# Chunked heads in pairs, unnormalised probabilities, outputs transposed on TensorE: one hybrid encoder layer

## The chip, the cores and the metric

The kernel runs on one NeuronCore of one Trainium2 chip. The metric is the device time of one execution in microseconds (us), the median of several runs. Five engines work side by side and meet only at semaphores: PE (TensorE: weight loads and matmuls), DVE (VectorE), ACT (ScalarE), POOL (GpSimd) and SP (SyncE), which here issues the DMA transfers.

## What is computed

One encoder layer over 1024 tokens of width 1024, all in float32. The mixer has two groups of eight heads. The latent group (MLA) has heads of 96 channels for query and key and sees all keys up to the query's chunk of 64 tokens. The chunked group (CA) has heads of 64 channels, sees a band of nine chunks and adds a bias by relative position. Both outputs are concatenated, projected and added to the residual; a gated MLP with a causal convolution follows.

```python
# latent heads, for a block of 128 queries
s = jnp.einsum('bqhd,bkhd->bhqk', qi, k, preferred_element_type=jnp.float32) * scale
s = jnp.where(mask[None, None], s, NEG_INF)          # key chunk <= query chunk
p = jax.nn.softmax(s, axis=-1).astype(v.dtype)
o = jnp.einsum('bhqk,bkhd->bqhd', p, v)
# chunked heads, for a chunk of 64 queries and its band of 576 keys
s = jnp.einsum('bqhd,bkhd->bhqk', qch, kb, preferred_element_type=jnp.float32) * scale + bias[None]
s = jnp.where(valid[None, None, None, :], s, NEG_INF)
p = jax.nn.softmax(s, axis=-1).astype(vb.dtype)
o = jnp.einsum('bhqk,bkhd->bqhd', p, vb)
mixed = jnp.dot(jnp.concatenate([o_mla, o_ca], axis=-1), w_out[l])
x = x + g_a[:, None, :] * mixed
```

## The kernel before

Every float32 product is made of three products of halves (hi*hi, hi*lo, lo*hi); `gemm3` (L144) issues them and its lines L148 to L150 stand for all large projections. `hi_of` (L73, on ACT at L75 or POOL at L77) and `lo_of` (L81, L82) split an operand. `scale_pool` (L70, L71) is POOL's multiplication by a column.

The kernel has four stages in time. First x is normalised and projected for the first head pair. Then the 64 query tiles of the chunked heads and the 64 of the latent heads run (128 queries of one head each), with other products between them. Then comes the output projection of the latent heads with the second norm (from L834), and last the MLP (from L887).

*The attention.* A `Unit` (L626) is four query tiles of one head: eight chunked heads and eight latent ones, in two halves g of the sequence, 32 units. `scores` (L634) makes the tile's score products (L656) in one of two PSUM tiles of tag "S" (two banks each); a chunked tile of the second half has 640 keys in two segments, six products, and one of the first half 128 to 512 keys, three products. Chunked heads lie on 64 partitions: head 2p on 0 to 63, head 2p+1 on 64 to 127 of the same page. DVE masks (L663, L674) and takes the minimum (L667, L671, L675), for scores carry a minus sign; ACT takes the exponential and its row sum (L681) into a tile of tag "P" (three buffers) or, if wider than 640, of tag "pg" (six, shared with other pages). DVE takes the reciprocal of the row sum and scales it (L683, L684). POOL writes the high half-precision part times that column (L698), DVE the low part (L701), both into one of three "HL" buffers; SP issues a transposing DMA (L703) into one of three "PT" buffers. `values` (L707) runs three tiles later (DEPTH): V, with hi and lo side by side in 128 columns, is stationary, the transposed probabilities move, and the result has the 64 channels (twice) on the partitions and 128 queries along the columns (L714). After four tiles ACT and DVE add the two halves with the scale of V undone (L721, L722), and SP stores 64 rows of 512 to DRAM (L723) as `oT_d`.

*The fill products.* The projections of the next pairs, the latent block, the up projections of the latent heads ("up0", "up1") and the chunked heads' output projection ("oca", `f_oca`, L596) are generators that `fill_step` (L777) advances; `pace` (L803) lets R_CA or R_MLA ns of fill run for each ns of attention, and `need` (L794) forces those that a unit must have. `gemm3_f` (L156) ties a fill product behind the attention's product of four entries ago in `trail` (LAG). `f_oca` loads the weights of one half of the columns, reads `oT_d` in slices of 128 tokens (L602), splits them on ACT and POOL (L603, L604) and keeps the result in DRAM (L609). The order on every engine is made by a planner that simulates a timeline; `high_priority` moves scores, splits and values ahead of fill.

*The output projection of the latent heads* (L855 on) reads `oT_d` in slices again (L858), splits them (L859, L860), multiplies, adds the kept part of the chunked heads (L868) and so on through the second norm.

`qk_page` (L612) transposes four token tiles on PE into a PSUM tile of tag "T" (one buffer), and ACT (L619 or L622) and DVE (L620 or L623) split it into a page of tag "Q" or "K".

## Time and profile before

| | us |
|---|---|
| median of 3 runs | 1521.95 |
| the runs | 1520.9, 1521.95, 1524.99 |
| span of the profiled execution | 1526.0 |
| score products of the chunked heads (L656) | 104.3 to 396.8 |
| score products of the latent heads (L656) | 433.0 to 660.0 |
| last products of probabilities and values (L714) | 681.0 |
| output projection of the latent heads on PE | 686.8 to 745.8 |
| first product of the MLP | 793.6 |

The profiled execution's own time is its span of 1526.0 us; it is a different execution from the three that were timed. The rows below give the DMA issues that the change touches: line of the program's transfer, count, size of one and median time from issue to landing.

```profile
wor<-w_out SPq DMA_DIRECT2D x16, 256.0 KB, 3.0
cl<-oT_d SPq DMA_DIRECT2D x16, 256.0 KB, 3.3
...
oT_d<-oc SPq DMA_DIRECT2D x16, 128.0 KB, 2.3
oT_d<-om SPq DMA_DIRECT2D x16, 128.0 KB, 2.5
ol<-oT_d SPq DMA_DIRECT2D x8, 256.0 KB, 4.0
PTm<-hlm SPq DMA_TRANSPOSE x88, 3.3
...
PTc<-hlc SPq DMA_TRANSPOSE x64, 3.4
```

Where the rows name tiles, c and m at the end tell chunked from latent heads: sc and sm are scores, Pc and Pm exponentials, hlc and hlm the half-precision parts, PTc and PTm their transposes, pvc and pvm the products with V, oc and om the outputs. Matmuls overlap in the rows, so the time that one holds PE is read from start to start, not from its length.

### The profile page before, as it was taken

Reading aid. Unit: us, or ns where it says so; the run is one execution under the profiler, and the core shown is the slowest. Engines: PE = TensorE matmul, PEld = TensorE weight load, DVE = VectorE, ACT = ScalarE, POOL = GpSimd, SP = SyncE. Lnnn points to the kernel's source line nnn. Section 1 sums busy time; section 2 is a strip of 40 time slices with the busy share of each in tenths; the row PEclk is TensorE's granted clock in tenths of the full one; section 3 lists DMA queues with packets and bytes.
Section 4 is the critical chain, followed back from the end, with each engine's and each line's share of the span. In section 5 each row is a group of like instructions: output and inputs, shape, how many; then the busy total and the mean of one; then the engine's idle time right before and its main releaser. Section 6 shows DMA issues by size and latency. Waiting matters only on the chain.

```text
span 1526.0 us, 19445 instructions
## 1 busy us (share of the span) xinstructions
PE 1338.1 (88%) x7100; PEld 1111.0 (73%) x7100; DVE 824.4 (54%) x1536; ACT 487.4 (32%) x919; POOL 664.7 (44%) x720
## 2 busy tenths in 40 slices
PE   3859989998767888858739999999999999999997
PEld 2749878987646666646528888888888888888885
DVE  6864786566768768843742433344334343434343
ACT  5443353343545545532413211212122121221200
POOL 5264463473799735435725231514314142341510
PEclk9979978989878899977859999999999999999998
DMA  7323657463613678787142110202112020110202
GB/s 270 133 67 73 138 119 142 121 131 94 122 40 70 150 143 174 165 181 247 56 138 69 56 55 28 70 30 67 42 42 69 15 83 28 56 56 28 70 1 110
DMA packets 202460, 142.90 MB, mean 94 GB/s; under 512 B 146294, under 2 KB 181242, under 8 KB 201340
## 3 DMA queue, kind: packets, MB, share of 16 engines
q1 hardware_dynamic: 202364, 141.66, 36.0%
q8 instruction: 56, 0.92, 0.3%
q14 instruction: 40, 0.33, 0.1%
HBM read 93.90 MB, written 13.11 MB: 70 GB/s over the span
## 4 chain that ended last, share of the span: by engine, by line
PE 63%; DMA 14%; DVE 10%; POOL 7%; issue 3%; ACT 2%; SPq 1%; POOLq 0%; DVEq 0%; ACTq 0%
PE up L148 10%; PE up L149 10%; PE up L150 10%; DMA aw<-w_ada 6%; PE dn L148 5%; PE dn L149 5%; PE dn L150 5%; DMA PTm<-hlm 4%; PE sc L656 2%; DVE adacc L241 2%; DVE aacc L428 1%; PE sm L656 1%; PE pvc L714 1%; POOL hlm L71 1%; DMA adaw<-w_ada 1%
## 5 line engine op out<-in xcount | busy, mean ns | idle before, releaser
L148 PE MATMUL up<-hT,wu_h 128*128 128x512 f32 x704 | 275.1, 391 | 0.0
L149 PE MATMUL up<-hT,wu_h 128*128 128x512 f32 x704 | 274.3, 390 | 0.0
L150 PE MATMUL up<-hT,wu_l 128*128 128x512 f32 x704 | 274.1, 389 | 0.0
L951 DVE TENSOR_TENSOR x<-x,dn 128x1024 f32<-128x1024 f32 x88 | 107.4, 1220 | 179.8 <-PE dn L150 179.8
L924 DVE SCALAR_TENSOR_TENSOR u<-up,pk,u 128x1023 f32<-128x1023 f32 x44 | 56.4, 1283 | 232.1 <-ACT u L923 232.1
L923 ACT ACTIVATE u<-up,pk 128x1024 f32<-128x1024 f32 x44 | 53.1, 1208 | 386.0 <-PE up L150 386.0
L149 PEld LDWEIGHTS up<-hT,wu_h 128*128 128x128 f32 x704 | 132.4, 188 | 28.0 <-issue 0.5
L148 PEld LDWEIGHTS up<-hT,wu_h 128*128 128x128 f32 x704 | 132.4, 188 | 27.9 <-issue 0.5
L82 POOL TENSOR_TENSOR wu_l<-wu_r,wu_h 128x1024 fp32r<-128x1024 f32 x44 | 105.7, 2402 | 107.9 <-PE up L149 60.1
L150 PEld LDWEIGHTS up<-hT,wu_l 128*128 128x128 f32 x704 | 132.4, 188 | 27.7 <-POOL wu_l L82 0.2
L77 POOL TENSOR_SCALAR wd<-wd_r 128x1024 fp32r<-128x1024 f32 x22 | 23.1, 1050 | 290.2 <-PE dn L150 289.1
L148 PE MATMUL dn<-wd,g 128*128 128x512 f32 x352 | 138.0, 392 | 5.0 <-ACT g L75 5.0
L149 PE MATMUL dn<-wd,g 128*128 128x512 f32 x352 | 137.9, 392 | 0.0
L150 PE MATMUL dn<-wd,g 128*128 128x512 f32 x352 | 137.4, 391 | 0.0
L71 POOL TENSOR_SCALAR hlm<-Pm,rim 128x512 f16<-128x512 f32 (+4 forms) x88 | 62.8, 717 | 69.1 <-DMA PTm<-hlm 46.6
L75 ACT ACTIVATE wu_h<-wu_r 128x1024 fp32r<-128x1024 f32 x44 | 46.5, 1057 | 141.1 <-DMA wu_r<-w_up 141.1
L938 POOL TENSOR_TENSOR wd_r<-wd_r,gmbc 128x1024 f32<-128x1024 f32 x22 | 52.6, 2392 | 80.6 <-DMA wd_r<-w_down 80.6
L701 DVE SCALAR_TENSOR_TENSOR hlm<-Pm,rim,hlm 128x512 f16<-128x512 f32 (+4 forms) x88 | 70.2, 801 | 31.7 <-POOL hlm L71 31.4
L148 PEld LDWEIGHTS dn<-wd,g 128*128 128x128 f32 x352 | 66.6, 189 | 19.4 <-issue 5.4
L71 POOL TENSOR_SCALAR hlc<-Pc,ric 128x640 f16<-128x640 f32 (+2 forms) x64 | 45.9, 719 | 78.5 <-DVE ric L684 38.9
L656 PE MATMUL sm<-mk,mq 96*128 96x512 f32 (+3 forms) x288 | 70.0, 375 | 9.8 <-ACT Pm L681 9.0
L656 PE MATMUL sc<-k,q 64*128 64x512 f32 (+3 forms) x288 | 71.2, 376 | 7.4 <-ACT Pc L681 4.9
(276 smaller groups left out, 3031.8 us busy)
## 6 DMA issues: line engine op xcount, KB each, us to landing
wu_r<-w_up SPq DMA_DIRECT2D x44, 512.0 KB, 3.6
aw<-w_ada SPq DMA_DIRECT2D x96, 128.0 KB, 2.2
wd_r<-w_down SPq DMA_DIRECT2D x22, 512.0 KB, 3.5
x<-x SPq DMA_DIRECT2D x16, 512.0 KB, 9.3
adaw<-w_ada_a SPq DMA_DIRECT2D x8, 1024.0 KB, 4.8
wq_r<-w_qk SPq DMA_DIRECT2D x32, 128.0 KB, 2.6
wor<-w_out SPq DMA_DIRECT2D x16, 256.0 KB, 3.0
cl<-oT_d SPq DMA_DIRECT2D x16, 256.0 KB, 3.3
```

What stands on the lines that cost most here:

```text
L71: pool.tensor_scalar(o, i, s, 1.0, op0=MUL, op1=MUL)
L75: act.activation(o, i, AF.Copy)
L82: (pool if eng == "p" else dve).tensor_tensor(o, i, f32(hi), op=SUB)
L148: pe.matmul(pt, sh, mh, start=(start and i == 0), stop=False)
L149: pe.matmul(pt, sh, ml, start=False, stop=False)
L150: pe.matmul(pt, sl, mh, start=False, stop=(stop and i == n - 1))
L656: last = pe.matmul(s[:, c:c + w], qpg[rs_, a, q], kpgs[kh][rs_, b, ko:ko + w], start=(a == 0 and b == 0), stop=(a == 1))
L701: dve.scalar_tensor_tensor(hl[:, w:2 * w], pp, ri[:], hl[:, :w], op0=MUL, op1=SUB)
L923: act.activation(u[:], pt[:], AF.Identity, scale=pk[:, cv + 2:cv + 3], bias=pk[:, cv + 3:cv + 4])
L924: dve.scalar_tensor_tensor(u[:, 1:], pt[:, :S - 1], pk[:, cv + 1:cv + 2], u[:, 1:], op0=MUL, op1=ADD)
L938: pool.tensor_tensor(raw[:], raw[:], gmbc[:], op=MUL)
L951: dve.tensor_tensor(x1[t][:], x1[t][:], pt[:], op=ADD)
```

## The change

- The two chunked heads of a pair now run together. `products` makes the score products of a tile as a generator, and the main loop takes one product of each head in turn; both score tiles of tag "S" are taken by one pair. `softmax` follows for one head and then the other. Values of chunked heads run one pair later (two entries in the queue), those of latent heads still three tiles later.
- The exponentials are split with the constant PSCALE; the division by the row sum moves behind the products with V.
- In `values` the transposed probabilities are stationary and V moves, so queries lie on the partitions. Four blocks of 128 columns (two heads by two tiles, or four tiles of a latent head) fill a "pv" tile; ACT copies the low halves, DVE adds the high ones, POOL multiplies with the reciprocals.
- When a pair of heads has its four tiles, `qk_page` transposes its output on PE, undoes the scale of V and splits it; the page (hi and lo, 512 KB) is stored. `f_oca` and the last output projection load such pages and split nothing. `f_oca` loads all its weights first and runs over tokens outside, columns inside.
- Tags: "P" 3 to 2 buffers, "PT" 3 to 4, "o" 1 to 3, "sq" joined to "R" (2 and 4 to 5 in all); pages of the outputs come from "K" and, when loaded, from "pg" or "ol". R_CA goes from 1.9 to 2.7, counted on half of a pair's product time.

Comments and the modes that the kernel did not use go too.

```diff
-P_BUFS, HL_BUFS, PT_BUFS, TB = 3, 3, 3, 1
-MODE_C = "1111"
-MODE_M = "1111"
+P_BUFS, HL_BUFS, PT_BUFS, TB = 2, 3, 4, 1
 PSCALE, VSCALE = 2.0 ** 15, 2.0 ** 14
-R_CA, R_MLA = 1.9, 0.5
+R_CA, R_MLA = 2.7, 0.5
...
-    oT_d = dram.tile([ND, P, S], F32, name="oT_d")
+    oT_d = [[dram.tile([P, 2, 512], F32, name=f"oT_d{k}_{h}") for h in range(2)] for k in range(ND)]
...
     def rtile(name, shape=(P, 512), dt=F32):
-        return apg.tile(list(shape), dt, name=name, tag="R", bufs=4)
+        return apg.tile(list(shape), dt, name=name, tag="R", bufs=5)
     def qtile(name):
-        return apg.tile([P, 512], F32, name=name, tag="sq", bufs=2)
+        return apg.tile([P, 512], F32, name=name, tag="R", bufs=5)
...
+    def load_oT(k, h, name):
+        pg = pgtile([P, 2, 512], F32R, name)
+        sp.dma_start(f32(pg[:]), oT_d[k][h][:])
+        return pg
     def f_oca():
-        for n in range(2):
-            ws = load_wo(4, n, "a", "p")
...
+        ws = [load_wo(4, n, "a", "p") for n in range(2)]
+        for h in range(2):
+            pgs = [load_oT(4 + k, h, f"ocl{k}_{h}") for k in range(4)]
+            for j in range(4):
+                sl = slice(j * P, (j + 1) * P)
+                for n in range(2):
+                    pt = ps.tile([P, 512], F32, name=f"oc{h}{j}_{n}", tag="mm", bufs=2)
+                    yield from gemm3_f(pt[:], [(pgs[k][:, 0, sl], pgs[k][:, 1, sl], ws[n][k][:, 0], ws[n][k][:, 1])
+                                               for k in range(4)])
+                    o = qtile(f"co{h}{j}_{n}")
+                    act.activation(o[:], pt[:], AF.Copy)
+                    sp.dma_start(part_d[4 * h + j][:, n * 512:(n + 1) * 512], o[:])
...
+        def products(u, i):
             qpg, kpgs = u.pages()
-            bias = u.bias() if u.band else None
             lo = max(0, i - 4) if u.band else 0
             n = (i - lo + 1) * P
+            s = ps.tile([P, 1024], F32, name=f"s{u.nm}_{i}", tag="S", bufs=2)
+            n0 = max(0, min(4, i + 1) - lo) * P
+            n1 = n - n0
+            c0 = 512 - n0 if n1 else 0
+            segs = [(c0, lo * P, n0, 0)] if n0 else []
+            if n1:
+                segs.append((512, max(lo, 4) * P - 512, n1, 1))
+            q = slice((i % 4) * P, (i % 4 + 1) * P)
+            rs_ = slice(u.base, u.base + u.rows)
+            u.s[i] = (s, c0, n, lo)
+            for a in range(2):
+                for c, ko, w, kh in segs:
+                    for b in range(2 - a):
+                        u.last = pe.matmul(s[:, c:c + w], qpg[rs_, a, q], kpgs[kh][rs_, b, ko:ko + w],
+                                           start=(a == 0 and b == 0), stop=(a == 1))
+                        yield max(107, w / 2.4)
...
+        def softmax(u, i):
+            bias = u.bias() if u.band else None
             nm = f"{u.nm}_{i}"
-            rsum = cst.tile([P, 1], F32, name=f"rs{nm}", tag="rsum", bufs=4)
-            ri = cst.tile([P, 1], F32, name=f"ri{nm}", tag="ri", bufs=4)
+            s, c0, n, lo = u.s.pop(i)
+            if i % 4 == 0:
+                u.rsum = cst.tile([P, 4], F32, name=f"rs{nm}", tag="rsum", bufs=4)
...
-                act.activation(pr[:, :n], sv, AF.Exp, bias=m[:], scale=-1.0, accum_out=rsum[:, 0:1])
+                act.activation(pr[:, :n], sv, AF.Exp, bias=m[:], scale=-1.0, accum_out=u.rsum[:, i % 4:i % 4 + 1])
             with tc.high_priority(offset=OFF_P):
-                dve.reciprocal(ri[:], rsum[:, 0:1])
-                dve.tensor_scalar(ri[:], ri[:], PSCALE, None, op0=MUL)
                 u.pt[i] = []
                 for x, (p0, p1) in enumerate(pieces):
                     w = p1 - p0
                     hl = at.tile([P, 1280], F16, name=f"hl{nm}_{x}", tag="HL", bufs=HL_BUFS)
                     pp = pr[:, p0:p1]
-                    cnt[0] += 1
-                    mode = (MODE_C if u.band else MODE_M)[cnt[0] % 4]
...
+                    scale_pool(hl[:, :w], pp, PSCALE)
+                    dve.scalar_tensor_tensor(hl[:, w:2 * w], pp, PSCALE, hl[:, :w], op0=MUL, op1=SUB)
                     tt = at.tile([P, 10, P], F16, name=f"PT{nm}_{x}", tag="PT", bufs=PT_BUFS)
                     sp.dma_start_transpose(tt[:, :2 * w // P, :], hl[:, :2 * w])
                     u.pt[i].append((tt, lo + p0 // P, w // P))
-            return sum(3 * max(107, w / 2.4) for _, _, w, _ in segs)
         def values(u, i):
-            if i % 4 == 0:
-                u.pv = ps.tile([P, 512], F32, name=f"pv{u.nm}_{u.g}", tag="pv", bufs=1)
-            c = slice((i % 4) * P, (i % 4 + 1) * P)
+            k = 2 * (i % 2) + u.odd if u.band else i % 4
+            if k == 0:
+                pvt[u.pair] = ps.tile([P, 512], F32, name=f"pv{u.nm}_{u.g}_{i}", tag="pv", bufs=1)
+            pv = pvt[u.pair]
+            c = slice(k * P, (k + 1) * P)
             todo = [(lo + j, tt[:, h * nk + j, :]) for tt, lo, nk in u.pt[i] for j in range(nk) for h in range(2)]
+            if (u.pair, u.g) not in opair:
+                opair[u.pair, u.g] = at.tile([P, 4, 2, 64], F32, name=f"o{u.nm}_{u.g}", tag="o", bufs=3)
+            o = opair[u.pair, u.g]
             with tc.high_priority(offset=OFF_V):
-                for x, (j, mov) in enumerate(todo):
-                    last = pe.matmul(u.pv[:, c], u.vst(j), mov, start=(x == 0), stop=(x == len(todo) - 1))
+                for x, (j, p) in enumerate(todo):
+                    last = pe.matmul(pv[:, c], p, u.vst(j), start=(x == 0), stop=(x == len(todo) - 1))
                 trail.append(last.ins)
-                if i % 4 == 3:
-                    sb = at.tile([P, 512], F32, name=f"sb{u.nm}_{u.g}", tag="sb", bufs=1)
...
+                if k == 3:
+                    if u.band:
+                        dst = o[:, i % 4 - 1:i % 4 + 1]
+                        v = pv[:].rearrange("p (t h a b) -> p t h a b", t=2, h=2, a=2)
+                        hi, lo = v[:, :, :, 0], v[:, :, :, 1]
+                        ri = cst.tile([P, 2, 2], F32, name=f"ri{u.nm}_{i}", tag="ri", bufs=4)
+                        for h, w in enumerate((u.mate, u)):
+                            dve.reciprocal(ri[:, :, h], w.rsum[:, i % 4 - 1:i % 4 + 1])
+                        rb = ri[:].unsqueeze(3).to_broadcast([P, 2, 2, 64])
+                    else:
+                        dst = o[:, :, u.odd]
+                        v = pv[:].rearrange("p (t a b) -> p t a b", t=4, a=2)
+                        hi, lo = v[:, :, 0], v[:, :, 1]
+                        ri = cst.tile([P, 4], F32, name=f"ri{u.nm}_{i}", tag="ri", bufs=4)
+                        dve.reciprocal(ri[:], u.rsum[:])
+                        rb = ri[:].unsqueeze(2).to_broadcast([P, 4, 64])
+                    act.activation(dst, lo, AF.Copy)
+                    dve.tensor_tensor(dst, dst, hi, op=ADD)
+                    pool.tensor_tensor(dst, dst, rb, op=MUL)
+            if i % 4 == 3 and u.odd:
+                pg = qk_page(lambda j: o[:, j].rearrange("p a b -> p (a b)"), f"oT{u.nm}_{u.g}", P, "K", 3, vscale[u.vs][1])
+                sp.dma_start(u.dst_d[u.g][:], f32(pg[:]))
             return 56 * len(todo)
-    cnt = [0]
+    pvt = {}
+    opair = {}
...
+    items = []
+    for p in range(4):
+        for g in range(2):
+            pair = [ca_unit(p, g, o) for o in range(2)]
+            pair[1].mate = pair[0]
+            items += [(pair, i) for i in range(4 * g, 4 * g + 4)]
+    for gr in range(2):
+        for hh in range(4):
+            for g in range(2):
+                u = mla_unit(gr, hh, g)
+                items += [([u], i) for i in range(4 * g, 4 * g + 4)]
+    queue = []
+    def pop_values():
+        u, i = queue.pop(0)
+        if i % 4 == 0:
+            need(u.needv)
+        pace(u.values(i), R_CA if u.band else R_MLA)
+    for us, i in items:
+        for u in us:
             if i % 4 == 0:
                 need(u.need)
                 u.prep()
-            pace(u.scores(i), R_CA if u.band else R_MLA)
-        if n >= DEPTH:
-            u, i = tiles[n - DEPTH]
-            if i % 4 == 0:
-                need(u.needv)
-            pace(u.values(i), R_CA if u.band else R_MLA)
+        cost = 0.0
+        with tc.high_priority(offset=OFF_S):
+            gens = [u.products(i) for u in us]
+            live = True
+            while live:
+                live = False
+                for g in gens:
+                    c = next(g, None)
+                    if c is not None:
+                        cost += c
+                        live = True
+            trail.append(us[-1].last.ins)
+        for u in us:
+            u.softmax(i)
+            queue.append((u, i))
+        pace(cost / len(us), R_CA if us[0].band else R_MLA)
+        while len(queue) > (2 if us[0].band else DEPTH):
+            pop_values()
+    while queue:
+        pop_values()
...
-        lo = gb.tile([P, 4, P], F32R, name=f"ol{t}", tag="ol", bufs=3)
-        hi = gb.tile([P, 4, P], F32R, name=f"oh{t}", tag="oh", bufs=3)
-        sp.dma_start(f32(lo[:]), oT_d[0:4, :, t * P:(t + 1) * P].rearrange("k p t -> p k t"))
-        hi_of("a", hi[:], f32(lo[:]))
-        lo_of("p", lo[:], f32(lo[:]), hi[:])
+        if t % 4 == 0:
+            oTs = []
+            for k in range(4):
+                pg = gb.tile([P, 2, 512], F32R, name=f"ol{k}_{t}", tag="ol", bufs=4)
+                sp.dma_start(f32(pg[:]), oT_d[k][t // 4][:])
+                oTs.append(pg)
+        sl = slice((t % 4) * P, (t % 4 + 1) * P)
         sp.dma_start(x1[t][:], I["x"][t * P:(t + 1) * P, :])
         pa = gb.tile([P, D], F32, name=f"pa{t}", tag="pa", bufs=4)
         sp.dma_start(pa[:], part_d[t])
         pt = ps2.tile([P, 1024], F32, name=f"op{t}", tag="op", bufs=3)
         for n in range(2):
             gemm3(pt[:, n * 512:(n + 1) * 512],
-                  [(hi[:, k], lo[:, k], wo[n][k][:, 0], wo[n][k][:, 1]) for k in range(4)])
+                  [(oTs[k][:, 0, sl], oTs[k][:, 1, sl], wo[n][k][:, 0], wo[n][k][:, 1]) for k in range(4)])
```

More of the change, by code (lines that the diff above doesn't have):

```diff
@@ L626, in layer_kernel, with __init__ @@
     class Unit:
-        def __init__(u, nm, base, rows, pages, vst, g, band, bias, odd, dst_d, vs):
+        def __init__(u, nm, base, rows, pages, vst, g, band, bias, odd, dst_d, vs, pair):
             u.nm, u.base, u.rows, u.pages, u.vst, u.g = nm, base, rows, pages, vst, g
-            u.band, u.bias, u.odd, u.dst_d, u.vs = band, bias, odd, dst_d, vs
-            u.pt = {}
-        def scores(u, i):
+            u.band, u.bias, u.odd, u.dst_d, u.vs, u.pair = band, bias, odd, dst_d, vs, pair
+            u.pt, u.s = {}, {}
@@ L810, in pace @@
             debt[0] -= c
-    units = [ca_unit(p, g, o) for p in range(4) for g in range(2) for o in range(2)]
-    units += [mla_unit(gr, hh, g) for gr in range(2) for hh in range(4) for g in range(2)]
-    tiles = [(u, i) for u in units for i in range(4 * u.g, 4 * u.g + 4)]
-    for n in range(len(tiles) + DEPTH):
-        if n < len(tiles):
-            u, i = tiles[n]
+    items = []
[17 more added lines that the diff above has]
+        for u in us:
             if i % 4 == 0:
```

46 lines of the change are left out of this document (2 added, 44 removed).

## The prediction

> **What bounds the kernel now.** I read the page first (busy shares, the 40 slices, the chain that ended last), then the stretches one by one, then the timelines and waits inside them. The span is 1526.0 us, 4.1 us above the median of the runs (1521.95), so sums are made against 1526 and 4 us are taken off at the end.
>
> ```profile
> PE 1338.1 (88%) x7100; PEld 1111.0 (73%) x7100; DVE 824.4 (54%) x1536; ACT 487.4 (32%) x919; POOL 664.7 (44%) x720
> ...
> PE   3859989998767888858739999999999999999997
> ...
> PEclk9979978989878899977859999999999999999998
> ...
> 104.00:398.00 294.00, 276.72 (x1947) 242.70 (x1946) 189.09 (x557) 119.85 (x324) 141.47 (x215) 0.92 0.54 117
> 398.00:433.00 35.00, 25.88 (x126) 20.27 (x125) 24.56 (x63) 18.66 (x44) 30.51 (x55) 0.77 0.32 69
> 433.00:505.00 72.00, 51.15 (x289) 40.89 (x287) 56.83 (x151) 41.56 (x101) 68.52 (x127) 0.82 0.34 73
> 505.00:662.00 157.00, 132.25 (x905) 104.46 (x905) 121.78 (x290) 77.80 (x164) 80.36 (x96) 0.96 0.76 159
> 662.00:687.00 25.00, 8.28 (x75) 7.00 (x72) 7.69 (x15) 6.64 (x12) 9.06 (x10) 0.59 0.88 199
> 687.00:746.00 59.00, 51.64 (x208) 40.93 (x209) 27.87 (x26) 15.77 (x26) 35.76 (x31) 0.85 0.51 176
> ```
>
> The last six rows are stretches: length, busy us of PE, weight loads, DVE, ACT, POOL, then clock, DMA share, GB/s. Chunked heads (104 to 398): PE is busy 277 of 294 us, so **PE bounds it**. From 398 to 505 POOL is busy 99 of 107 us: **POOL bounds** the up projections. From 505 to 662 (latent heads with the chunked heads' output projection) no engine is full. The MLP, from 793 on, is PE at 9 in every slice and is not touched.
>
> **Score products of two heads side by side.** The edit issues the two heads' products in turn. Their operands lie on 64 partitions each, one head on 0 to 63, the other on 64 to 127.
>
> ```profile
> 142.90 0.60 PE L616 MATMUL k_ps<-ident,qn 128*128 128x128 f32 x4
> ...
> 158.42 1.24 PE L656 MATMUL sc<-k,q 64*128 64x512 f32 x6
> 159.60 0.73 PE L714 MATMUL pvc<-PTc,v 128*128 128x128 f16 x10
> 160.14 0.36 PE L149 MATMUL ipq<-wq_s,hT 128*128 128x256 f32 x1
> 160.34 0.28 PE L150 MATMUL ipq<-wq_s,hT 128*128 128x256 f32 x1
> 160.55 1.14 PE L656 MATMUL sc<-k,q 64*128 64x384 f32 x6
> 161.62 0.39 PE L148 MATMUL ipq<-wq_s,hT 128*128 128x256 f32 x1
> ```
>
> From start to start a tile's six products hold PE 1.18 us (158.42 to 159.60) and 1.07 us (160.55 to 161.62). A 256-column product elsewhere takes 0.12 us, so 1920 columns would need about 0.9 us: some 0.2 to 0.3 us is spent entering and leaving the 64-row form. The eight tiles of a head take, read the same way at full clock, 0.48, 0.55, 0.72, 0.89, 1.18, 1.07, 1.07 and 1.23 us: 7.19 us, times 8 heads 57.5 us. No row shows two heads' products together. Least gain: they do not overlap, and only one of two entries is saved, 32 x 0.27 = 8.6 us. Most: a pair costs what a tile costs, 28.8 us. The form 64*128 says that each product uses half of the array's rows, so I take overlap, but bound it by weight loads: the transposes in the first row are four short products, one every (0.60 - 0.27) / 3 = 0.109 us, though 128 columns stream in half of that. Twelve products then need 1.31 us, six 0.65: a pair of heads takes 0.65 + 0.65 + 0.72 + 0.89 + 4 x 1.31 = 8.15 us, four pairs 32.6. Saved: **24.9 us** at full clock, 27 at the stretch's 0.92.
>
> The Trainium skill (TensorE: Matmul & The Clock Gate, Part 3: Packing small matmuls) says that products in different row groups run at once, about 4 ns apart, and that a weight load overlaps a running product only where its row group differs. By it a pair would cost about one tile, the 28.8 us above; no run here shows it yet.
>
> **Softmax.** Two DVE instructions per tile go (L683 0.155 us, L684 0.148 us): 128 x 0.303 = 38.8 us, a link between exponential and POOL's split. The splits take a constant in place of a column, priced at no change. The new reciprocals, 48 at 0.155, add 7.4 us.
>
> **Values and their way out.** Stationary and moving change places, with the same count of 128x128 half-precision products, 0.056 us each; nothing. Per block of four, 32 times, ACT 0.68 (L721) and DVE 0.74 (L722) on 64 rows become an ACT copy of 256 columns (0.47, as L408), a DVE sum (0.48, as L409) and a POOL product. The last lies between 0.48 (128 columns, L465) and 1.06 (512 columns, L371); I take 0.75, 24 us in all. Then 16 pages of four transposes on PE (0.109 each, 7 us), ACT 0.68 and DVE 0.74 (as L622, L623). DVE changes by -38.8 + 7.4 - 23.7 + 15.4 + 11.8 = -28 us; ACT by -21.8 + 15 + 10.9 - 15.1 (the splits of cl and ol, 24 x 0.63) = -11.
>
> The o transposes **add a wait**: PE is in order, and every fill product and score behind them waits for ACT, DVE and POOL, up to 0.47 + 0.48 + 0.75 = 1.7 us, 16 times, 27 us at worst; nothing at best. The q and k transposes (L616) already wait so: 53 us of idle time ahead of them, counted on PE and on its weight loads, so 26; 18 of that is for POOL before the first heads and in the up projections, which leaves 8 us over 48 groups. For 16 groups I take 3 us, half in each phase.
>
> **Queue and loads.** SP drops 32 stores (0.46 us) and 24 loads (0.53 and 0.39), and issues 16 stores and 16 loads of 512 KB. Between 505 and 662 that is 8 fewer loads and 8 fewer stores, some 8 us of a queue that spends 1.24 us on each DMA transpose.
>
> ```profile
> L71 POOL TENSOR_SCALAR hlm<-Pm,rim 128x512 f16<-128x512 f32 (+4 forms) x67 | 47.8, 716 | 64.2 <-DMA PTm<-hlm 42.1 <-DVE sm L674 4.7 <-DVE mm L675 4.7
> L82 POOL TENSOR_TENSOR cl<-cl,ch 128x512 fp32r<-128x512 f32 x16 | 20.7, 1293 | 10.7 <-ACT ch L75 9.0 <-PE pvm L714 1.8
> ```
>
> POOL stands idle 42 us until a transpose has emptied one of three HL buffers: that **ring** paces this stretch (64 pieces, 157 / 64 = 2.45 us each, 7.4 us round). Its count stays at three. What shortens a round is DVE's 0.303 us on 48 tiles and SP's 8 us, a third of each (three buffers): 4.9 + 2.8 = 8 us. Probability buffers get fewer (P from 3 to 2; the wide ones share six page tiles with the oT loads), so the bounds are 0 and 15.
>
> **Sum.** 104 to 398: -27 + 3.5 (transposes) + 1.5 (waits) = **-22**. DVE loses work there and POOL, 48% busy, hides its products; without that cover they would cost 12 us. 398 to 505: POOL gets about four products on the path, **+3**. 505 to 662: **-8**; the transposes hide in PE's 16% idle time. 662 to 687: the last page is needed only at t=4: 0. 687 to 746: POOL loses 8 x 1.28 us, about three of them on the chain (-4), but four pages of 512 KB must land before t=0 is done, against 256 KB and a split (6.3 us): some 10 us, +4: **0**, between -6 and +8. Together -27: 1526 - 27 = 1499, less 4: **1495 us**; with the terms' own bounds 1480 to 1510.
>
> **Rivals.** *No overlap* on PE: the first stretch gains 8.6 - 5 = 3.6, in all -3.6 + 3 - 8 = -9: 1513 us. For it: no row shows overlap. Against: the half-array form.
>
> *More than forecast*: full overlap, and idle (17 us) and lost clock (8% of 294, 23 us) halved since PE waits less: -28.8 - 20 + 5 = -44 there, -15 at the ring, -6 behind: 1526 - 62 = 1464, less 4, 1460 us. For it: DVE is relieved throughout. Against: PE with less to do waits more, not less, and the clock rows fall where PE waits.
>
> *Slower: the score buffers.* There are two; a pair takes both, so the next pair's products wait until both exponentials have read.
>
> ```profile
> ACT Pc L681 <- DVE mc L671: 67.9, 25, 8.2
> POOL hlc L71 <- DVE ric L684: 36.2, 16, 7.3
> ```
>
> A turn is products 1.3, DVE 1.3 for each head (memset, two reductions, readout), exponential and its readout 1.0: 4.9 us, under the 294 / 32 = 9.2 us that a pair has now. But ACT waited for DVE's minimum up to 8.2 us, because DVE works in order. If two splits (1.9), a page (1.4) and a fill (1.6) stand ahead, a turn is 9.8 us and the stretch 314: +20, and with +3 - 8 in all 1541, less 4: 1537 us. It decides from 9.2 us a turn. Against: DVE is busy 64% there. The Trainium skill (TensorEngine Tiling (Array Packing), PSUM Bottleneck) warns of just this: packing speeds the array, not the emptying of PSUM.
>
> **How the numbers follow.** Forecast 0.50, more 0.17, no overlap 0.13, slower 0.20. 0.3% (4.6 us, about the spread of the three runs) is what counts as a difference. Faster: 0.50 + 0.17 + 0.10; same: 0.03 from no overlap and 0.03 from a mild form of the slower case; slower 0.17. The range 1458 to 1532 takes in the two milder cases and reaches into the slower one. The forecast's own range is 1480 to 1510.
>
> **What will show it.** Right: pairs of score products starting nearly together, a group of 12 within 1.4 us; the chunked stretch near 272 us; POOL's wait for the PTm transposes still largest after 505. Wrong: groups of 12 over 2 us; PE idle over 30 us before the latent heads with ACT waiting for DVE's minimum; PE waiting for POOL at the o transposes; a gap at t=4 of the output projection.

## The result, and the profile after

| | before | after |
|---|---|---|
| median of 4 runs, us | 1523.08 | 1563.41 |
| span of the profiled execution | 1526.0 | 1562.2 |
| chunked heads' score products | 104.3 to 396.8 | 101.7 to 411.9 |
| latent heads' score products | 433.0 to 660.0 | 451.0 to 704.9 |
| last product of probabilities and values | 681.0 | 718.4 |
| first product of the MLP | 793.6 | 829.6 |

The kernel became slower by 2.66% (ratio 1.0266, 95% interval 1.0251 to 1.0282), some 40 us, where 27 us of gain were forecast. The stretches of the kernel after (length, busy us of PE, weight loads, DVE, ACT, POOL, then clock, DMA share, GB/s):

```profile
102.00:413.00 311.00, 279.06 (x1999) 244.70 (x1998) 184.71 (x477) 121.31 (x335) 148.44 (x232) 0.91 0.54 118
413.00:451.00 38.00, 26.24 (x124) 21.01 (x122) 22.71 (x54) 18.48 (x45) 29.87 (x59) 0.78 0.20 43
451.00:537.00 86.00, 61.81 (x308) 47.56 (x309) 57.75 (x122) 41.85 (x101) 79.94 (x139) 0.82 0.40 105
537.00:705.00 168.00, 133.57 (x918) 106.52 (x917) 104.48 (x215) 69.26 (x153) 46.84 (x77) 0.93 0.64 139
705.00:726.00 21.00, 8.48 (x76) 6.21 (x74) 8.17 (x15) 7.92 (x14) 8.96 (x10) 0.69 0.94 270
726.00:783.00 57.00, 50.88 (x218) 41.64 (x219) 31.09 (x27) 11.77 (x19) 26.97 (x23) 0.90 0.56 214
```

The chunked stretch is 18 us longer (311 against 293) with DVE less busy (185 against 189). The latent stretch, 451 to 718, is 19 us longer than 433 to 681. In its second part, 537 to 705, POOL, whose ring was to pace it, is busy 47 of 168 us. The MLP is unchanged.

First the edit itself. PE's timeline after, one pair at 640 keys (start, length in us, then the operation):

```profile
154.68 1.14 PE L654 MATMUL sc<-k,q 64*128 64x384 f32 x6
155.75 0.39 PE L147 MATMUL ipq<-wq_s,hT 128*128 128x256 f32 x1
...
156.53 1.14 PE L654 MATMUL sc<-k,q 64*128 64x384 f32 x6
157.60 0.39 PE L146 MATMUL ipq<-wq_s,hT 128*128 128x256 f32 x1
```

The two heads' products are not together. Each head's six go when its own "S" tile is free, 1.07 us each from start to start, as before. In the program's order on PE only 55 of the 288 chunked score products are followed at once by one of the other head (none before). The planner reorders what the loop issues; issuing in turn does not keep a turn. 46 of the 55 are in the first tile of a half. Some narrow tiles stand next to each other as two blocks, three products of one head and then three of the other, and four of these five groups overlap as well, for instance:

```profile
350.34 0.80 PE L654 MATMUL sc<-k,q 64*128 64x384 f32 x6
351.07 0.40 PE L714 MATMUL pvc<-v,PTc 128*128 128x128 f16 x4
```

Six products of 384 columns take 0.73 us here, where three of one head took 0.72 before. So the two heads' products need not alternate; they have to be neighbours and ready at once. Summed from start to start, chunked score products hold PE 68.3 us before and 58.9 after.

DVE's longest waits between 102 and 413 us, in the kernel after (who waits, for what: total us, times, longest), and then those of SP's queue:

```profile
DVE aacc L426 <- DMA aw<-w_ada: 60.8, 41, 3.9
DVE hlc L696 <- POOL hlc L69: 14.5, 21, 1.8
```

```profile
SPq L422 <- DMA aw<-w_ada: 44.0, 28, 3.5
SPq L698 <- DVE hlc L696: 29.4, 29, 5.5
SPq L422 <- DVE aacc L426: 17.1, 29, 1.8
```

`f_ada`, a side chain that forms the other modulation rows, loads 96 weight tiles into the ring "A". It has three buffers, one of which holds the sum, so two loads are in flight. DVE stands 61 us behind them (before: 42, shown below), with the softmax queued behind it, and SP 61 us (before: 45), with the P transposes behind it.

### The profile page after: what moved, and what is told of

Its sections match the earlier page's. It is cut to its first block, busy times and chain, and to the rows that moved or that the text cites. A ratio compares the mean times of both kernels' runs of the same rounds, so it can differ in the third digit from the quotient of the medians.

```text
span 1562.2 us, 19299 instructions
## 1 busy us (share of the span) xinstructions
PE 1347.5 (86%) x7164; PEld 1116.3 (71%) x7164; DVE 800.1 (51%) x1344; ACT 476.1 (30%) x911; POOL 640.2 (41%) x728
## 4 chain that ended last, share of the span: by engine, by line
PE 65%; DMA 12%; POOL 9%; DVE 8%; issue 3%; ACT 2%; SPq 1%; DVEq 0%; POOLq 0%; ACTq 0%
PE up L147 10%; PE up L146 10%; PE up L148 10%; PE dn L146 5%; PE dn L147 5%; PE dn L148 5%; DMA aw<-w_ada 4%; DMA PTm<-hlm 4%; PE sc L654 2%; PE sm L654 2%; DVE adacc L239 1%; PE ipq L148 1%; PE ipq L146 1%; PE pvc L714 1%; DVE aacc L426 1%
## 5 line engine op out<-in xcount | busy, mean ns | idle before, releaser
L69 POOL TENSOR_SCALAR hlm<-Pm 128x512 f16<-128x512 f32 (+4 forms) x88 | 51.7, 593 | 98.6 <-ACT Pm L688 49.4
L654 PE MATMUL sm<-mk,mq 96*128 96x512 f32 (+3 forms) x288 | 74.8, 388 | 14.6 <-ACT Pm L688 8.4
L426 DVE SCALAR_TENSOR_TENSOR aacc<-aw,cs,aacc 128x256 f32<-128x256 f32 x84 | 47.0, 560 | 65.5 <-DMA aw<-w_ada 65.1
L146 PEld LDWEIGHTS dn<-wd,g 128*128 128x128 f32 x352 | 66.6, 189 | 19.4 <-issue 5.4
L714 PE MATMUL pvm<-vt,PTm 128*128 128x128 f16 x576 | 50.7, 235 | 34.2 <-DMA PTm<-hlm 31.9
L148 PEld LDWEIGHTS dn<-wd,g 128*128 128x128 f32 x352 | 66.6, 189 | 14.0
```

Of the source, the lines that this page charges most:

```text
L69: pool.tensor_scalar(o, i, s, 1.0, op0=MUL, op1=MUL)
L146: pe.matmul(pt, sh, mh, start=(start and i == 0), stop=False)
L148: pe.matmul(pt, sl, mh, start=False, stop=(stop and i == n - 1))
L426: dve.scalar_tensor_tensor(acc[:], w[:], cs[:, k:k + 1], acc[:], op0=MUL, op1=ADD)
L654: u.last = pe.matmul(s[:, c:c + w], qpg[rs_, a, q], kpgs[kh][rs_, b, ko:ko + w], start=(a == 0 and b == 0), stop=(a == 1))
L714: last = pe.matmul(pv[:, c], p, u.vst(j), start=(x == 0), stop=(x == len(todo) - 1))
```

## The experiments

**Pages, and alternation.** `e1_ocl_own` reads the chunked outputs back into the dead tiles of V; `e2_chain` ties each product of a pair behind the last one; `e3_both` does both; `e4_by_tile` issues the two heads tile by tile.

```diff
 e1, e3
-        pg = pgtile([P, 2, 512], F32R, name)
+        pg = apg.tile([P, 2, 256], F32R, name=name, tag="v16", bufs=6)
...
 e2, e3
+                    with (tc.issue_after(prev.ins) if prev else nullcontext()):
                         c = next(g, None)
...
 e4
-            items += [(pair, i) for i in range(4 * g, 4 * g + 4)]
+            items += [([u], i) for i in range(4 * g, 4 * g + 4) for u in pair]
...
```

> The kernel after, with the chunked heads' transposed outputs read back (ocl) into half-size tiles of the long dead v buffers instead of the six page tiles that the wide probabilities of the latent heads use. Page theory: in the kernel after, the first ocl loads took page tiles from 476 us on, the wide tiles of the first latent head stood still from 477 to 497 us, and the latent stretch never made up for it; so here the stretch 451 to 718 us loses 20 to 27 us and the time is 1537 to 1544 us. Rival, POOL theory: the latent stretch is late because POOL got more work (output products, 8 weight splits at once); then the time stays within 4 us of 1563 us. The chunked stretch (102 to 412 us) should not change under either.

> The kernel after, with each of a pair's twelve score products tied behind the one before it on PE, so that the planner cannot pull the two heads apart (226 instead of 55 neighbours of different heads among the 288 products). Lost-alternation theory: score groups shrink from about 61 us to about 35 us, and the chunked stretch (310 us) gets 15 to 25 us shorter, the time 1540 to 1548 us. Rival, score-buffer theory: the first product of a pair now waits for both buffers, PE stands idle in their place (32 us idle before 412 us grows by as much as the groups shrink), and the time is 1560 us or more.

> Both edits of the two runs before. If the losses are separate (page theory and lost-alternation theory both right) the gains add: 1515 to 1528 us, no slower than the kernel before (1523 us). If only pages matter, 1540 us; if neither, 1563 us.

> The kernel after, with the two heads' tiles issued one after the other (six products, softmax, six products, softmax) instead of twelve products and two softmaxes; same rate of fillers. If issuing pairs as such delays the chunked stretch (both exponentials due together, two DVE chains behind each other), the stretch shortens from 310 us by 5 to 15 us though it loses the overlap of the narrow tiles (about 6 us): 1550 to 1560 us. If the pairing is not the cause of the late chunked stretch, it gets 5 to 10 us longer: 1568 to 1573 us.

Measured: 1555.6, 1556.3, 1546.0 and 1563.1 us. The page theory gets 8 of its 20 us or more, the chain 7 of 15 or more, and the two about add, at least 18 us short of what was expected of both. Where `e1` gains does not fit its theory: 6 us lie in the chunked stretch (101 to 405), which should not have changed, and 3 in the latent one. Issuing by tile leaves the total as it was, outside both expected ranges: the chunked stretch is 7 us shorter, and the rest gives it back. So pairing as such explains little of the 40 us. The chain itself does what it should on PE, in the timeline of `e2_chain`:

```profile
153.38 0.43 PE L654 MATMUL sc<-k,q 64*128 64x384 f32 x1
153.74 0.39 PE L147 MATMUL ipq<-wq_s,hT 128*128 128x256 f32 x1
...
155.13 1.14 PE L654 MATMUL sc<-k,q 64*128 64x384 f32 x11
156.20 0.39 PE L148 MATMUL ipq<-wq_s,hT 128*128 128x256 f32 x1
```

One product goes ahead as soon as its tile is free; the other eleven take 1.07 us, what six took alone. Score products now hold PE 45.9 us, 22.4 less than before and 13 less than as built. The stretch falls by 13 us to 298, still above the 293 of before. PE stands idle 36 us in it (32 as built, 17 before), 24 of these ahead of the values, for the transposes of P (7 as built, 9 before). So PE's work alone does not set the stretch.

**Small edits on top of `e3_both` (1546.0 us).**

```diff
 e5_dve_product
-                    pool.tensor_tensor(dst, dst, rb, op=MUL)
+                    dve.tensor_tensor(dst, dst, rb, op=MUL)
 e6_p3_pt3
-P_BUFS, HL_BUFS, PT_BUFS, TB = 2, 3, 4, 1
+P_BUFS, HL_BUFS, PT_BUFS, TB = 3, 3, 3, 1
 e7_queue3
-        while len(queue) > (2 if us[0].band else DEPTH):
+        while len(queue) > (3 if us[0].band else DEPTH):
 e8_rate31
-R_CA, R_MLA = 2.7, 0.5
+R_CA, R_MLA = 3.1, 0.5
```

> The kernel of the run with both edits (own space for ocl, chained score products; 1546 us), with the product of each output block by the reciprocal row sums moved from POOL to DVE. In that kernel POOL, which works in order, stood 30 us behind 'the sum on DVE' at these products after 517 us, while splits for the next tiles queued behind it. Head-of-line theory: without them in POOL's queue the ring of splits turns faster, the latent stretch loses 12 to 25 us, the time is 1521 to 1534 us. Rival: POOL's wait only stands in for another (its splits would have waited for ACT's exponentials or the HL buffers anyway): within 4 us of 1546 us.

> The same kernel of 1546 us with three narrow probability buffers and three PT buffers, as before, instead of two and four. If the exponentials wait for a free P buffer (POOL's waits for the exponential, 51 us after 517 us against almost none before), 5 to 12 us are gained: 1534 to 1541 us. If PT buffers matter more in the chunked stretch, where values wait 24 us for the transposes, it gets 3 to 8 us slower. If neither ring binds, within 3 us.

> The same kernel of 1546 us with three instead of two tiles left in the queue between softmax and values in the chunked heads. With the products chained PE waited 24 us for the transposes of P ahead of the values between 104 and 412 us, against 9 us in the kernel before. Queue theory: one more tile of distance takes away 10 to 15 us of it and the time falls to 1531 to 1538 us. Rival: the four PT buffers then hold up the transposes instead, or PE waits at the next place; within 4 us of 1546 us.

> The same kernel of 1546 us with the rate of fill products in the chunked heads raised from 2.7 to 3.1. If the saved PE time is lost because nothing fills it (PE idle 42 us between 104 and 412 us against 19 us before), more fill between scores and values covers the waits for the transposes and brings the up projection forward: 1534 to 1541 us. If the stretch is bound by the chain through DVE, the exponentials come later by as much as the fill takes: 1544 to 1550 us.

Measured: 1546.7, 1551.2, 1541.9 and 1555.9 us. Three of the four ideas miss: POOL's products behind the sums cost nothing that can be seen, a third P buffer doesn't pay for the PT buffer, and more fill makes it 10 us slower. Only the queue gives 4 us, and these are not clear of noise (runs of 1540.4 to 1546.0 against 1542.5 to 1547.7). Tuning what the change had set did not find the loss.

**The side chain.** `e9`, `e10` and `e11` leave out 84 of its 96 loads in the kernel before, the kernel after and `e7_queue3`, and use one tile eight times (so the modulation rows come out different). `e13_after_ahead` makes all loads, a step ahead, in five buffers (and two "o" tiles for three).

```diff
 e9, e10, e11
-                    w = atile(f"aw{m}_{n}_{k}")
-                    sp.dma_start(w[:], I["w_ada"][k * P:(k + 1) * P, c0:c0 + 256])
+                    if k == 0:
+                        w = atile(f"aw{m}_{n}_{k}")
+                        sp.dma_start(w[:], I["w_ada"][k * P:(k + 1) * P, c0:c0 + 256])
 e13
-        return apg.tile([P, 256], F32, name=name, tag="A", bufs=3)
+        return apg.tile([P, 256], F32, name=name, tag="A", bufs=5)
...
+                    if k % 2 == 0:
+                        ahead(2)
+                    w = aws.pop(0)
...
-                opair[u.pair, u.g] = at.tile([P, 4, 2, 64], F32, name=f"o{u.nm}_{u.g}", tag="o", bufs=3)
+                opair[u.pair, u.g] = at.tile([P, 4, 2, 64], F32, name=f"o{u.nm}_{u.g}", tag="o", bufs=2)
```

> The kernel before, in which the side chain of the modulation rows loads one of its eight weight tiles per column block and uses it eight times (84 of 96 loads left out; rows 2, 3 and 4 of the modulation come out different; DVE's work stays). In the kernel before DVE stood 49 us behind these loads (aw) between 104 and 412 us, and they hold 24% of the chain of waits from 100 to 440 us. Side-chain theory: this chain and not PE sets the length of the chunked stretch, so it gets 15 to 35 us shorter and the time is 1488 to 1508 us. Rival, PE theory (the prediction's reading): PE is busy 277 of 294 us there, so at most its 17 idle us can go: 1510 to 1523 us.

> The same omission in the kernel after (84 of 96 loads of the side chain left out). DVE stood 64 us behind these loads between 104 and 412 us there. If the loads are what the change makes worse (more waiting in front of the exponentials), the difference between after and before, 40 us, shrinks here by 10 us or more: at least 25 us faster than 1563 where the kernel before gains 15. If they cost both kernels alike, the difference stays near 40 us.

> The same omission in the best kernel so far (ocl in its own space, chained score products, three tiles in the queue; 1542 us). Here the score products hold PE 23 us less than before, so if the side chain's loads are what hides that gain, this kernel gains 10 us more by the omission than the kernel before does, 25 to 45 us: 1497 to 1517 us, and its chunked stretch becomes the shorter of the two by 10 to 20 us. If another wait (the transposes of P) takes their place, it gains no more than the kernel before.

> The kernel after with the side chain's 96 loads all made, but each pair issued one step ahead, into a ring of five buffers instead of three (paid for with one of three o buffers). Queue theory: the kernel after loses its time because DVE, and the load queue in front of the P transposes, stand behind loads of which only two are in flight; then most of the 38 us that leaving out the loads gave comes back here: 1528 to 1540 us, the chunked stretch below 295 us. Traffic theory: the loads' share of the DMA engines costs the time, so issuing them earlier gives little: 1555 to 1565 us.

Measured: 1516.6, 1525.0, 1525.7 and 1535.8 us. The loads cost the kernel before 7 us and the kernel after 38. Made ahead, they all stay and 28 us come back: ratio to before 1.0088 (1.0066 to 1.0109). So most of the loads' cost is the waits and not the traffic. The kernel before with its loads a step ahead was not run; by `e9` some 7 us could be won there.

The omission shortens the chunked stretch by 15 us in `e9` and by 30 in `e10`, and the time ahead of it by 11 and 8; the latent stretch takes 12 and 11 back (248 to 260 us, 267 to 278). The chunked stretch in `e9`, then in `e10`:

```profile
93.00:371.00 278.00, 268.66 (x1983) 240.15 (x1983) 196.90 (x567) 123.09 (x331) 151.63 (x222) 0.95 0.45 93
```

```profile
94.00:375.00 281.00, 270.71 (x2020) 240.11 (x2018) 183.82 (x486) 123.06 (x343) 155.34 (x240) 0.94 0.48 99
```

So without these waits the change leaves the stretch about as long as it was (278 and 281 us). Nor is it shorter in `e11`, where the products are chained: 284 us. `e11` was expected 25 to 45 us below 1542 and gained 16. The stretches of `e13_after_ahead`, and its SP queue's waits from 98 to 381 us:

```profile
98.00:381.00 283.00, 268.80 (x2001) 237.35 (x1999) 180.25 (x465) 120.18 (x334) 148.76 (x232) 0.94 0.56 127
381.00:420.00 39.00, 26.55 (x127) 21.56 (x127) 23.76 (x58) 18.67 (x47) 30.74 (x62) 0.78 0.20 43
420.00:685.00 265.00, 206.82 (x1292) 161.06 (x1290) 171.05 (x354) 112.58 (x257) 128.60 (x220) 0.86 0.59 132
```

```profile
SPq L709 <- DVE hlc L707: 38.9, 28, 7.6
SPq L748 <- DVE oTc L636: 22.7, 3, 15.4
...
SPq L423 <- DVE aacc L437: 12.7, 24, 1.7
```

The chunked stretch falls from 311 to 283 us, below the 293 of the kernel before; the wait for the loads is gone from SP's list but for 13 us.

**All edits together, and one part alone.** `e12_wo_spread` (on `e7_queue3`) makes the eight weight splits of `f_oca` one at a time and raises the rate of fill in the latent heads from 0.5 to 0.6 for it. `e14_ahead_ocl_wo` is `e13` with ocl apart and the weights spread; `e15_ahead_chain` has the chain and the longer queue as well. `e16_before_undivided` is the kernel before without L683 and L684, split by PSCALE, its output rows undivided.

```diff
 e12, e14, e15
-R_CA, R_MLA = 2.7, 0.5
+R_CA, R_MLA = 2.7, 0.6
...
-        ws = [load_wo(4, n, "a", "p") for n in range(2)]
+        ws = [[], []]
+        for n in range(2):
+            for k in range(4, 8):
+                ws[n] += load_wo(k, n, "a", "p", 1)
+                yield 1000
...
 e16
-                dve.reciprocal(ri[:], rsum[:, 0:1])
-                dve.tensor_scalar(ri[:], ri[:], PSCALE, None, op0=MUL)
...
```

> The kernel of 1542 us with the eight weight tiles of the chunked heads' output projection split one by one among the latent tiles (and the rate of fillers there raised from 0.5 to 0.6 to pay for it), instead of all eight in a row. In all kernels made from the change the exponentials of the latent heads stand still for 13 to 20 us between the 16th and the 17th tile, while POOL makes the eight splits of 1.27 us; in the kernel before, which makes four at a time, they don't. Burst theory: 8 to 14 us are gained, 1528 to 1534 us. Rival: POOL has to make them all anyway and the wait only moves: within 4 us of 1542 us.

> The run before this one with ocl in its own space and the eight weight tiles of the output projection spread (no chain, two tiles in the queue). If the losses are separate, 10 to 15 us less than the run before it: 1515 to 1528 us. If the latent stretch takes back what the chunked stretch gives, as it did when the loads were left out (it grew from 268 to 279 us), no more than 5 us less.

> The same as the run before this one with the score products chained and three tiles in the queue. Without the loads' waits the chained kernel's chunked stretch was 3 us longer than the one whose planner was free (285 against 282 us), though its score products hold PE less. If the chain's gain was only cover for other waits, this run is 0 to 10 us slower than the run without chain; if the forecast's 25 us come out once nothing else waits, it is 8 to 20 us faster.

> The kernel before with one part of the change alone: the two small DVE instructions per tile (reciprocal and scaling) left out, the split by a constant, so that the rows of the attention's output stay undivided by their sums. By the prediction DVE has 39 us less to do and the ring of splits turns faster: 5 to 10 us in the latent stretch, perhaps some more in the chunked one: 1508 to 1518 us. Rival: DVE's time there is cover under the side chain's loads and the transposes, within 4 us of 1523 us.

Measured: 1541.4, 1524.4, 1522.7 and 1525.2 us. Spreading the weights gives nothing: the burst theory falls. `e14` and `e15` reach the kernel before (ratios 1.0017, 0.9999 to 1.0036, and 1.0007, 0.9986 to 1.0028). The undivided split alone gives nothing (1.0015, 1.0002 to 1.0029). In `e15` the chunked stretch is 274 us (280 in `e14`), but the latent one takes back what was won. The execution profiled here took 1531 us, 8 above the median of its kernel:

```profile
99.00:373.00 274.00, 255.06 (x1997) 224.52 (x1997) 179.90 (x463) 118.89 (x333) 146.11 (x231) 0.95 0.57 134
373.00:414.00 41.00, 27.28 (x130) 21.40 (x128) 24.75 (x60) 19.64 (x48) 31.63 (x64) 0.76 0.28 62
414.00:683.00 269.00, 209.76 (x1283) 168.72 (x1284) 171.52 (x347) 113.36 (x256) 130.87 (x221) 0.82 0.58 124
```

**The pages of the latent outputs.** Where the latent stretch loses time is seen on PE in the kernel after, at the end of a pair of heads:

```profile
588.35 1.61 PE L654 MATMUL sm<-mk,mq 96*128 96x512 f32 x6
590.52 0.72 PE L714 MATMUL pvm<-vt,PTm 128*128 128x128 f16 x10 [0.56 <-DVE om L733]
591.36 0.66 PE L618 MATMUL oTm_ps<-ident,om 128*128 128x128 f32 x4
...
595.90 0.50 PE L146 MATMUL oc<-wo,ocl 128*128 128x512 f32 x1 [2.35 <-DMA ocl<-oT_d]
...
596.69 0.64 PE L618 MATMUL mq_ps<-ident,qn 128*96 128x128 f32 x4
...
600.01 0.86 PE L618 MATMUL mk_ps<-ident,kn 128*96 128x128 f32 x4
...
601.64 0.49 PE L654 MATMUL sm<-mk,mq 96*128 96x128 f32 x2
```

and the last reading of the output's page, in DVE's rows:

```profile
594.89 0.75 DVE L625 SCALAR_TENSOR_TENSOR oTm<-oTm_ps,vabm,oTm 128x512 fp32r<-128x512 f32 x1
```

Last value products, the output's transposes (oTm), then the next head's q page (mq), then its k page (mk), and only then scores: 11.7 us without a latent score product. Four transposes took the "T" bank from 591.36 to 595.64, until DVE, which had splits to make first, had read it. They are not the only wait in this hole: PE also stands 2.35 us for an `ocl` load. Such holes of over 6 us add up to 85 us in the kernel after; five of the seven, at 530.9 (19.4 us long), 590.0, 605.6, 650.5 and 664.9 us, lie around an oTm. Before they were 48. All three kinds of page use the one "T" bank and the three "K" or two "Q" pages. `e17_no_latent_page` is `e15` without the latent outputs' pages, which are stored untransposed; `e18_all_dve` is `e15` with the products of `e5`.

```diff
 e17
-            if i % 4 == 3 and u.odd:
+            if i % 4 == 3 and u.odd and not u.band:
+                for a in range(2):
+                    sp.dma_start(u.dst_d[u.g][:, a], o[:].rearrange("p t a b -> p (t a b)"))
+            elif i % 4 == 3 and u.odd:
                 pg = qk_page(lambda j: o[:, j].rearrange("p a b -> p (a b)"), f"oT{u.nm}_{u.g}", P, "K", 3, vscale[u.vs][1])
```

> The kernel with all edits (loads ahead, ocl in its own space, weights spread, products chained, three in the queue; 1523 us), with the transposes of the latent heads' outputs and their split into pages left out: the rows go to memory as they are, in two stores of 256 KB per block (the output projection then reads them untransposed). Left out are 8 groups of four PE transposes (3.5 us), 8 ACT and 8 DVE readings. Page theory: these share the one transposing PSUM bank and the three K pages with the next head's q and k; without them the latent stretch falls from about 265 to 250 us, the time to 1508 to 1514 us. Rival: they cost no more than their PE time: 1518 to 1524 us.

> The same kernel with all edits, with the products by the reciprocal sums on DVE instead of POOL. At 1546 us this move gave nothing. If POOL's 33 us behind the sums count now that the other waits are gone, 5 to 10 us are gained: 1513 to 1518 us, faster than the kernel before (1523 us). If POOL would wait for the exponentials anyway: 1520 to 1526 us.

Measured: 1490.3 us (ratio 0.9777, 0.9739 to 0.9816) and 1528.7 us. Eight groups of four transposes (3.5 us of PE) with one reading each on ACT (0.69 us) and DVE (0.75 us) are worth 32 us; this is far more than even the page theory had put down. The products on DVE gain nothing; the 6 us that they cost by the medians are not clear of noise (ratio to before 1.0041, 1.0021 to 1.0060, against `e15`'s 1.0007). Stretches of `e17`, and then some of its waits from 484 to 642 us:

```profile
98.00:374.00 276.00, 256.52 (x1999) 225.06 (x1998) 180.33 (x464) 119.35 (x334) 146.49 (x232) 0.94 0.57 134
374.00:414.00 40.00, 26.72 (x128) 21.34 (x128) 24.14 (x59) 19.36 (x47) 30.88 (x62) 0.79 0.27 60
414.00:642.00 228.00, 184.11 (x1257) 148.02 (x1256) 167.09 (x342) 108.27 (x250) 134.19 (x221) 0.90 0.68 148
```

```profile
POOL hlm L69 <- DMA PTm<-hlm: 43.5, 28, 4.9
...
POOL hlm L69 <- ACT Pm L704: 13.4, 8, 4.0
...
ACT mk L640 <- PE mk_ps L634: 10.0, 5, 2.8
```

The same waits in `e15`, 490 to 683 us:

```profile
POOL hlm L69 <- DMA PTm<-hlm: 45.9, 19, 6.1
POOL hlm L69 <- ACT Pm L704: 44.8, 22, 5.8
POOL om L750 <- DVE om L749: 32.6, 7, 8.7
...
ACT mk L640 <- PE mk_ps L634: 24.9, 10, 4.3
...
ACT mq L637 <- PE mq_ps L634: 14.3, 7, 4.9
```

The first two stretches are nearly equal in both; the third goes from 269 to 228 us (more than the 32 us of the medians, since `e15`'s execution was a long one). Without the pages ACT no longer waits 14 us for the q transposes, waits 10 instead of 25 us for those of k, and POOL 13 instead of 45 us for exponentials. The holes over 6 us shrink from 74 to 25 us.

## Why the prediction was wrong

**What bounds the chunked stretch** is the step that failed first. "PE bounds it" rested on 277 busy of 294 us. Busy is not bound. In the trace of before, loads of the side chain hold 26.6% of the chain of waits from 104 to 398 us, more than any other entry (the score products 12.2%), and DVE stood 42 us behind them. The views of before, the chain of this stretch and the wait:

```profile
by line: DMA aw<-w_ada 26.6%; PE sc L656 12.2%; PE pvc L714 5.4%; DVE aacc L428 5.2%; PE ipq L148 4.1%; PE ipq L149 3.8%; PE ipq L150 3.6%; PE ipv L148 3.3%; PE ipv L149 3.3%; PE ipv L150 3.1%; DVE hlc L701 2.9%; issue 2.8%; DMA PTc<-hlc 2.
```

```profile
DVE aacc L428 <- DMA aw<-w_ada: 42.4, 41, 3.2
```

The prediction names neither, though the wait is the row between the two waits that it shows under the *slower* rival (67.9 and 36.2 us). `e13` shows that the loads count in the kernel after: a step ahead, they let this stretch go from 311 to 283 us. But the share of the chain is not what they are worth. 26.6% of the stretch before is 78 us, and without 84 of the 96 loads it is 15 us shorter (`e9`); in the kernel after the share is only 17.1%, and the same omission takes 30 us off (`e10`).

**The score products, −27.** That two heads' products overlap was right, and so was the size on PE; the premise was wrong that the pair stays together, and so was the step from PE's time to the stretch. Chained, the products hold PE 22.4 us less (forecast 24.9 at full clock, 27 at the granted one); as built, 9.4. The bound by weight loads (1.31 us for twelve) was too careful: eleven took 1.07 us. The rule of the Trainium skill that the prediction weighed (TensorE: Matmul & The Clock Gate, Part 3: Packing small matmuls) holds in these rows. The chain saves 13 us of PE against the kernel as built. The stretch gets shorter by 13 us from the kernel after to `e2`, by 5 from `e1` to `e3`, by 6 from `e14` to `e15`, and longer by 3 from `e10` to `e11` (the last two pairs differ in the queue too, and the last in ocl; each figure is from one execution). The stretch of 272 us that was to show the forecast right appears as 274 us in `e15`, but most of that is the loads': the kernel before without them takes 278.

**The o transposes, +3 of up to 27.** PE's wait at the transposes themselves is small, as forecast (0.4 us for oTc and 3.2 for oTm in the kernel after, 2.6 of these at the last page). But the step looked only at what PE waits for there. What is late next is the following head's q and k page, with its scores, exponentials and splits behind it: 32 us for the eight latent pages in `e17`, above the 27 us that were called the worst. The eight chunked pages were not tried apart.

**Page tiles.** "The wide ones share six page tiles with the oT loads" was named, but only widened a bound. Apart, they save 8 us (`e1`); since 6 of these lie in the chunked stretch, it is not shown that the shared tiles cost them.

**Softmax and ring, −8.** The undivided split alone moves nothing (`e16`). The pacing by POOL's ring does not hold after the change: POOL waits most for exponentials (49 us against 34 for the PTm transposes after 537). Without the latent pages that wait falls from 45 to 13 us (`e17`), and the transposes lead again.

**Right:** POOL's products cost nothing that can be seen (`e5`); the last stretches change by about a microsecond; no gap at t=4. The *slower* rival had the sign but not the mechanism: score products waited 6.9 us for exponentials in the kernel after, 4.9 before, so the two score buffers decide nothing. Its sign, PE idle over 30 us with ACT waiting for DVE's minimum, did appear (32 us idle), but ACT's wait got shorter, 57 us against 68. A range that ended at 1532 us had no case for the loads and the pages at once.

The sum of the parts is not exact: 28 us (loads, `e13`), 8 (`e1`) and the latent pages' 32 were each taken in another kernel, and together they exceed 40. The planner orders the whole anew for each edit, and some of a difference of a few microseconds may be its doing.

**Open:** why the same loads hold the kernel after back more than the one before (argued: a pair's two softmaxes stand behind one stalled DVE); and whether bank "T", the "K" pages or the order that the planner gives them is what holds the next head. A bank or page of its own for the outputs was not tried. What takes the loads' place in the chunked stretch, once they are gone, and keeps it at 274 to 284 us is not settled either. No version that computes everything beat the kernel before; `e15` equals it.

## What to carry to other kernels

Read the chain of waits and the load queue inside the stretch that is to gain before calling an engine its bound: 94% busy can still be held up by a two-deep ring of loads. Then leave the suspect out, for its share of the chain is not its price. Price a transposition added to PE by what must follow it (readings, a bank, a page, the next user of both), not by its own columns. And where a planner orders the instructions, an order that matters has to be tied down, and then looked up in the program.

## What the hardware showed

- Two row groups run wholly side by side: eleven products of 64 rows in 1.07 us, against six of one head in 1.07 us, and for narrow tiles two heads' six products in 0.56 us against 0.55 for three of one. They do not have to alternate: three and three in blocks took 0.73 us, against 0.72 for three.
- Of 32 us that the pages of `e17` were worth, only 3.5 are PE's work. The granted clock moved with the gaps: 0.82 in `e15`'s latent stretch, 0.90 in `e17`'s, with PE's work the same but for those transposes. Of the 41 us between these two stretches 15 are less idle time of PE, and 26 less busy time.
